# Late key weights and output weights of the first layer: split beside the projections and kept in scratch, in place of split beside the attention

## The chip, the cores and the metric

The program runs on one core of a Trainium2 chip. The metric is the device time of one execution in microseconds; before the change it is 3276.54 us, the median of three runs from 3276.2 to 3276.81 us. A profiled execution is one more run, in which a hardware profiler records the start and end of each instruction on the tensor engine (PE, with its weight loads as PEld), the vector engine (DVE), the scalar engine (ACT), GpSimd (POOL) and the queues that issue transfers; nearly all of these stand on the queue of SyncE (SP).

## The reference

A streaming encoder with two layers takes 2048 prompt rows and 64 sample rows of 1024 numbers, in 16 heads of 64. Layer A is attention over a band of 576 positions with a softmax; layer B is a strictly causal stick-breaking attention. What the change touches is the first layer's projection and its gated output:

```python
def a_project(x, g, w_in):
    h = rms_norm(x, g)
    q, k, v, gate = jnp.split(h @ w_in, 4, axis=-1)
    return split_heads(q), split_heads(k), split_heads(v), gate

def gated_out(o, gate, w_out):
    b, t = o.shape[:2]
    return (o.reshape(b, t, D_MODEL) * jax.nn.silu(gate)) @ w_out
...
            op = chunk_band_prompt(qp, kp, vp, rel_bias_a[i])
            xp = xp + gated_out(op, gp, w_out_a[i])
```

All is in 32-bit floats.

## The kernel before

**Numbers in two parts.** The matrix products run in a 32-bit matmul format of lower precision. Each operand is cut into a head, which that format holds, and a rest, the difference; a product is head by head, head by rest and rest by head. A cut is one ACT instruction (the head) and one DVE instruction (the rest): `split` (L209), or `scaled_split` (L213), which multiplies the weights by the norm's gains and goes through a 128x1024 block of weights in eight pieces of 128x128.

**Four stages.** Layer A's projections (values first, then keys, queries and gates by pairs of heads, 24 jobs), layer A's attention, layer B's projections, layer B's attention. In the trace the keys of layer A begin at 213 us, its attention runs from about 689 to 1300 us, layer B's projections to about 2020 us, and layer B's attention to the end.

**Beside the projections** (`projections`, L239) small staged tasks are handed out to the 24 jobs (`stages.pop(0)`): they cut caches and value differences and write them to scratch in device memory. In layer A they are 56: 8 caches, 8 biases, 32 value differences, 8 blocks of layer B's cached keys. In layer B they end with 16 `stage_w_out` tasks (L486), which load half of a 128-row block of layer B's output weights, cut it, and store head and rest.

**Late work beside the attention.** Products that the first items of the attention do not need are put off. `DEFER` (L42) names them: layer A's keys, layer B's gates and queries, for the second half of the prompt. `late_job` (L736) makes one such product for one pair of heads: `load`, for layer A also the four `cut` steps, then two chunks of matmuls into `ps_j`, their cut into `sp` and stores, and for some chunks a sum `lkn` (on POOL) with its turn to rows. `lkn` takes over a buffer of `sp`, so it waits until stores of `sp` have landed. After the late jobs come eight `w_out_steps` (L805) that fill the two big tiles with the output weights, then `out_steps`. The class `Beat` (L900) weaves them in: one beat is one tile of scores, and `RATE` 0.4 steps of late work fall on a beat of layer A.

**Where the weights come from** depends on `KEPT = "b"` (L43). For layer B, `projections` stores the cut weights of `DEFER` to scratch right after the cut (L381), `late_job.load` fetches head and rest, and `w_out_steps` fetches the pieces that `stage_w_out` left. For layer A, `late_job.load` fetches the weights as they are (`lraw`, 512 KB) and `cut` makes `lwh` and `lwl` beside the attention; `w_out_steps` fetches `woraw` (512 KB) for each of eight blocks and cuts it into the big tiles.

**What sets the order.** A list scheduler fixes each engine's order from a model of times; during the attention the steps of late work that stand in `in_place` keep their program order. At run time each engine, and SP's queue too, goes strictly in its order: a load that waits for its buffer, or for an earlier transfer, holds every transfer behind it.

Of the kernel before, what the change touches and what calls it, by code (L numbers as in the profile page):

```python
# [9 lines left out]
F32 = mybir.dt.float32  # L10
F32R = mybir.dt.float32r
# [5 lines left out]
P = 128  # L17
D = 1024
NK = D // P
# [13 lines left out]
CH = 512  # L33
# [6 lines left out]
SAMPLE = {(1, 0): [4, 3], (3, 2): [2, 1, 0]}  # L40

DEFER = dict(a=[("k", hp) for hp in range(HP)], b=[(k, hp) for k in "gq" for hp in range(HP)])  # L42
KEPT = "b"  # L43

RATE = dict(a=0.4, b=0.3)
LAG = dict(a=3, b=5)
# [4 lines left out]
STEP = 2  # L51
# [19 lines left out]
def f32(ap):  # L71
    return ap.bitcast(F32)
# [28 lines left out]
def encoder_step(ctx: ExitStack, tc: tile.TileContext, a: dict, o: dict):  # L101
    nc = tc.nc
# [39 lines left out]
    dram = ctx.enter_context(tc.tile_pool(name="scratch", bufs=1, space=DRAM))  # L142
# [5 lines left out]
    opool = ctx.enter_context(tc.tile_pool(name="out", bufs=1))  # L148
# [7 lines left out]
    def big_pair():  # L156
        return [big.tile([P, NK, D], F32R, name=f"big{i}", tag=f"big{i}") for i in range(2)]
# [13 lines left out]
    lay = {}  # L171
    for L, rows in (("a", CACHE_A), ("b", PAST)):
        lay[L] = dict(


            q=[dram.tile([3, P, T], F32R, name=f"q_{L}{i}") for i in range(HP)],
            k=[dram.tile([2, P, T + rows], F32R, name=f"k_{L}{i}") for i in range(HP)],

            v=dram.tile([T + rows, H, P], F32R, name=f"v_{L}"),
            g=[dram.tile([P, T], F32, name=f"gate_{L}{i}") for i in range(HP)],  # L180

            o=[dram.tile([HP, P, CH if g < GROUPS else NS], F32, name=f"o_{L}{g}") for g in range(GROUPS + 1)],

            w={x: dram.tile([2, P, NK, P], F32R, name=f"w_{L}{x[0]}{x[1]}") for x in DEFER[L] if L in KEPT},
        )

    vraw = dram.tile([1 + T, D], F32, name="v_raw")
    x1d = dram.tile([T, D], F32, name="x1")

    wod = [dram.tile([P, 2, D], F32R, name=f"wo_{k}") for k in range(NK)]  # L190
# [18 lines left out]
    def split(hi, lo, src):  # L209
        act.activation(hi, src, AF.Copy)  # L210
        dve.tensor_tensor(lo, src, f32(hi), ALU.subtract)

    def scaled_split(hi, lo, src, g):  # L213
        for k in range(src.shape[1]):
            act.activation(hi[:, k], src[:, k], AF.Copy, scale=g[:, k : k + 1])
            dve.scalar_tensor_tensor(lo[:, k], src[:, k], g[:, k : k + 1], f32(hi[:, k]), ALU.mult, ALU.subtract)
# [278 lines left out]
    def stage_bias(hp, pool):  # L495
# [231 lines left out]
    def job_steps(L, jobs, x2, first, prompt):  # L727

        return [
            late_job(L, *job, hp, x2, first, prompt)  # L730
            for hp in range(HP)
            for job in jobs
            if (job[0], hp) in DEFER[L]
        ]

    def late_job(L, kind, w, c0, g, hp, x2, first, prompt):  # L736
# [60 lines left out]
        behind = []  # L797
# [4 lines left out]
        cuts = [] if L in KEPT else [partial(cut, k0) for k0 in range(0, NK, STEP)]  # L802
        return [in_place(x) for x in [load] + cuts], products, behind

    def w_out_steps(src, w):  # L805

        raws = {}
# [10 lines left out]
        def load(k):  # L818
            if k < NK:
                tag = ("oh", "ol")[k % 2]  # L820
                raws[k] = opool.tile([P, D], F32, name="woraw", tag=tag, bufs=2)
                sp.dma_start(raws[k], src[k * P : (k + 1) * P])
# [9 lines left out]
        return [  # L832
            (
                [in_place(partial(load, i)) for i in range(3)] if k == 0 else [],
                [None],
                [[in_place(partial(cut, k)), in_place(partial(load, k + 3))]],
            )
            for k in range(NK)
        ]

    def out_steps(L, g, w, residual, done):

# [225 lines left out]
    staged_b += [partial(stage_w_out, k, half) for k in range(NK) for half in range(2)]  # L1068
# [18 lines left out]
    with (  # L1087
# [11 lines left out]
        beat.beside += w_out_steps(a["w_out_a"][0], w_out)  # L1099
        order.on = False  # L1100

        def done_a(t, n, xr, c):
# [160 lines left out]
    with (  # L1263
# [46 lines left out]
        beat.beside += w_out_steps(None, w_out)  # L1310
# [235 lines left out]
```

## Time and profile before

| | |
|---|---|
| median of 3 runs | 3276.54 us |
| profiled execution, span | 3278.2 us |
| PE busy | 3204.2 us, 98% |
| DVE busy | 1887.0 us, 58% |
| ACT busy | 1711.4 us, 52% |
| POOL busy | 1291.4 us, 39% |
| moved by transfers | 688.41 MB, mean 210 GB/s |
| mean granted PE clock | 0.994 |

The profiled execution is 1.7 us longer than the median of the runs. A share of busy time is a mean over four stages; in the projections PE is busy without a gap, in the attention ACT and DVE work beside it at about four fifths of the time. The end of a matmul is modelled and matmuls overlap, so a busy PE says only that it had work; its idle time and its clock say what was lost. In the view of windows each row gives busy microseconds and instructions of each engine, the granted clock, the busy share of the 16 DMA engines and their rate.

### The profile page before, as it was taken

How to read it: one execution, taken by the hardware profiler on the slowest of the kernel's cores; microseconds unless marked ns; L12 is line 12 of the kernel's file. 1: busy time of each engine (PE TensorE's matmuls, PEld its weight loads, DVE VectorE, ACT ScalarE, POOL GpSimd, SP SyncE). 2: the span in 40 equal slices, each digit the busy share in tenths (PEclk: the TensorE clock that was granted, in tenths of full speed). 3: DMA queues.
4: the chain of work that ended last, by engine and by line, in shares of the span. 5: the costliest groups of instructions: out<-in, count | busy, mean ns of one | idle time of the engine just before them, and what ended most of it. 6: DMA issues, size and time to landing. Idle time of an engine off the chain costs nothing.

```text
span 3278.2 us, 53687 instructions
## 1 busy us (share of the span) xinstructions
PE 3204.2 (98%) x17928; PEld 2791.0 (85%) x17928; DVE 1887.0 (58%) x3786; ACT 1711.4 (52%) x3719; POOL 1291.4 (39%) x1950
## 2 busy tenths in 40 slices
PE   8999999999998999999999999999999989999999
PEld 7889999988887898878889998788888878888877
DVE  4235431147778775231044333788878878888873
ACT  5234222258888776143134442566666656666662
POOL 3001110026665554020044200444477766877761
PEclk9999999999999999999999999999999999999999
DMA  6359993387899983553399999977735566455423
GB/s 202 121 185 368 349 331 118 117 237 220 240 260 267 252 237 130 164 174 128 113 357 352 348 357 328 251 217 217 213 121 148 162 203 174 124 143 141 138 72 119
DMA packets 464892, 688.41 MB, mean 210 GB/s; under 512 B 51446, under 2 KB 261398, under 8 KB 464615
## 3 DMA queue, kind: packets, MB, share of 16 engines
q1 hardware_dynamic: 405158, 633.85, 61.8%
q10 hardware_dynamic: 59456, 51.13, 4.8%
q8 instruction: 143, 2.34, 0.3%
q14 instruction: 135, 1.10, 0.1%
HBM read 408.78 MB, written 276.07 MB: 209 GB/s over the span
## 4 chain that ended last, share of the span: by engine, by line
PE 75%; issue 7%; DVE 6%; DMA 6%; ACT 2%; POOL 2%; SPq 1%; POOLq 0%; ACTq 0%; DVEq 0%
PE ps_t L90 23%; PE ps_v L90 11%; PE acc L90 10%; PE z L90 9%; PE wt L90 8%; PE ps_j L90 6%; PE ps_o L90 5%; DVE s L90 3%; DVE pl L90 2%; DMA vt<-v_b 1%; PE ps_tr L90 1%; ACT ph L90 1%; DMA kt<-k_b 1%; POOL s L90 1%; ACT s L90 1%
## 5 line engine op out<-in xcount | busy, mean ns | idle before, releaser
L90 DVE TENSOR_TENSOR pl<-wt,ph 128x512 fp32r<-128x512 f32 (+1 forms) x864 | 551.9, 654 | 122.4 <-ACT ph L90 118.7
L90 ACT ACTIVATE ph<-wt 128x512 fp32r<-128x512 f32 (+1 forms) x864 | 485.7, 578 | 205.4 <-PE wt L90 178.2
L90 PE MATMUL ps_t<-x_own,wh 128*128 128x362 f32 (+1 forms) x2304 | 567.5, 327 | 0.0
L90 PE MATMUL wt<-ident,s 128*128 128x128 f32 x3472 | 551.5, 274 | 13.4 <-DVE pl L90 6.8
L90 PEld LDWEIGHTS wt<-ident,s 128*128 128x128 f32 x3472 | 418.6, 141 | 88.3 <-DVE pl L90 12.9
L90 ACT ACTIVATE f<-z 128x512 f32<-128x512 f32 (+4 forms) x680 | 355.1, 535 | 196.1 <-PE z L90 139.7
L90 PEld LDWEIGHTS ps_t<-x_own,wh 128*128 128x128 f32 x2304 | 405.0, 188 | 1.8
L90 POOL TENSOR_TENSOR s<-f,s 128x256 f32<-128x256 f32 x416 | 361.3, 870 | 104.2 <-DVE s L90 95.9
L90 PE MATMUL acc<-ph,vt 128*128 128x512 f32 (+3 forms) x1088 | 376.2, 381 | 14.1 <-DMA vt<-v_b 7.5
L90 PE MATMUL z<-kt,q 128*128 128x512 f32 (+3 forms) x1280 | 375.4, 381 | 12.9 <-DMA q<-q_b 5.8
L90 PE MATMUL ps_t<-x_own,wl 128*128 128x362 f32 (+1 forms) x1152 | 376.7, 327 | 0.0
L90 PE MATMUL acc<-pl,vt 128*128 128x512 f32 (+3 forms) x1088 | 364.6, 368 | 7.2 <-DVE pl L90 6.8
L90 POOL TENSOR_SCALAR s<-s,rc 128x640 f32<-128x640 f32 (+5 forms) x264 | 199.2, 760 | 387.3 <-DMA keys<-k_a 193.3
L90 PE MATMUL ps_o<-big,oh 128*128 128x512 f32 x1088 | 336.2, 392 | 0.2 <-ACT oh L90 0.2
L90 POOL TENSOR_TENSOR two<-f 128x256 f32<-128x256 f32 x416 | 259.5, 626 | 166.3 <-ACT f L90 150.0
L90 DVE TENSOR_TENSOR_SCAN s<-two,s,own 128x256 f32<-128x256 f32 x408 | 299.7, 738 | 33.6 <-POOL two L90 32.3
L90 PEld LDWEIGHTS z<-kt,q 128*128 128x128 f32 x1280 | 221.9, 192 | 43.5 <-ACT f L90 11.8
L90 PE MATMUL ps_j<-big,lwh 128*128 128x512 f32 x768 | 246.9, 397 | 1.1 <-DVE pl L90 0.6
L90 PE MATMUL ps_t<-big,wh 128*128 128x512 f32 x768 | 238.9, 391 | 0.0
L90 PEld LDWEIGHTS ps_o<-big,oh 128*128 128x128 f32 x1088 | 202.2, 188 | 41.3 <-ACT oh L90 0.4
L90 PEld LDWEIGHTS acc<-ph,vt 128*128 128x128 f32 x1088 | 198.7, 192 | 37.1 <-ACT ot L90 8.4
L90 DVE CUSTOM_DVE_ANT_0 s<-z,bias 128x640 f32<-128x640 f32 (+4 forms) x256 | 184.7, 733 | 77.2 <-PE wt L90 51.1
(148 smaller groups left out, 5528.9 us busy)
## 6 DMA issues: line engine op xcount, KB each, us to landing
vt<-v_b SPq DMA_DIRECT2D x80, 512.0 KB, 4.9
v_b<-vs SPq DMA_DIRECT2D x64, 512.0 KB, 5.7
q<-q_a SPq DMA_DIRECT2D x128, 256.0 KB, 5.9
q<-q_b SPq DMA_DIRECT2D x128, 256.0 KB, 4.6
vt<-v_a SPq DMA_DIRECT2D x48, 512.0 KB, 7.1
kt<-k_b SPq DMA_DIRECT2D x96, 256.0 KB, 5.6
keys<-k_a SPq DMA_DIRECT2D x80, 256.0 KB, 7.1
v_a<-vs ACTq DMA_DIRECT2D x32, 512.0 KB, 2.7
```

What stands on the lines that cost most here:

```text
L90: ins = op(*args, **kwargs)
```

## The change

The distinction by `KEPT` goes: both layers keep cut weights in scratch. Beside layer A's projections the weights of the eight late keys are stored after their cut (16 stores of 512 KB), and 16 tasks `stage_w_out` for layer A's output weights are added to the staged ones, which are now 72 on 24 jobs. Beside layer A's attention a late job loads head and rest (two loads of 512 KB in place of one) and has no `cut`; a step of `w_out_steps` is two loads of 512 KB into the big tiles, in place of one load of 512 KB and two cuts of 128x512.

```diff
-KEPT = "b"
...
-            w={x: dram.tile([2, P, NK, P], F32R, name=f"w_{L}{x[0]}{x[1]}") for x in DEFER[L] if L in KEPT},
+            w={x: dram.tile([2, P, NK, P], F32R, name=f"w_{L}{x[0]}{x[1]}") for x in DEFER[L]},
...
-    def stage_w_out(k, half, pool):
+    def stage_w_out(L, k, half, pool):
         raw = pool.tile([P, CH], F32, name="vcur", tag="vr", bufs=2)
         cols = slice(half * CH, half * CH + CH)
-        nc.sync.dma_start(raw, a["w_out_b"][0][k * P : (k + 1) * P, cols])
+        nc.sync.dma_start(raw, a[f"w_out_{L}"][0][k * P : (k + 1) * P, cols])
         vs = pool.tile([P, 2, CH], F32R, name="vs", tag="vs", bufs=2)
         split(vs[:, 0], vs[:, 1], raw)
-        nc.sync.dma_start(f32(wod[k][:, :, cols]), f32(vs))
+        nc.sync.dma_start(f32(wod[L][k][:, :, cols]), f32(vs))
...
         def load():
-            if L not in KEPT:
-                st["raw"] = opool.tile([P, NK, P], F32, name="lraw", tag="og", bufs=1)
-                c = c0 + hp * P
-                sp.dma_start(st["raw"], w[:, c : c + P].rearrange("(k p) c -> p k c", p=P))
             st["wh"] = opool.tile([P, NK, P], F32R, name="lwh", tag="oh", bufs=2)
             st["wl"] = opool.tile([P, NK, P], F32R, name="lwl", tag="ol", bufs=2)
-            if L in KEPT:
-                for i, part in enumerate((st["wh"], st["wl"])):
-                    sp.dma_start(f32(part), f32(lay[L]["w"][kind, hp][i]))
-
-        def cut(k0):
-            ks = slice(k0, k0 + STEP)
-            scaled_split(st["wh"][:, ks], st["wl"][:, ks], st["raw"][:, ks], g[:, ks])
+            for i, part in enumerate((st["wh"], st["wl"])):
+                sp.dma_start(f32(part), f32(lay[L]["w"][kind, hp][i]))
...
-        return [in_place(x) for x in [load] + cuts], products, behind
+        return [in_place(load)], products, behind
...
         def parts(k):
             if k == 0:
                 w.extend(big_pair())
             for i in range(2):
-                sp.dma_start(f32(w[i][:, k]), f32(wod[k][:, i]))
-
-        if src is None:
-            return [([], [None], [[in_place(partial(parts, k))]]) for k in range(NK)]
+                sp.dma_start(f32(w[i][:, k]), f32(wod[L][k][:, i]))
...
-        def cut(k):
-            if k == 0:
-                w.extend(big_pair())
-            for c in range(0, D, CH):
-                cols = slice(c, c + CH)
-                split(w[0][:, k, cols], w[1][:, k, cols], raws[k][:, cols])
-            del raws[k]
...
+    staged += [partial(stage_w_out, "a", k, half) for k in range(NK) for half in range(2)]
```

The scheduler makes a new order from it. Three places matter below. In the rows, a line number one smaller is only the line that went with `KEPT`.

The first is POOL at the start of layer A's attention (`s` is a tile of softmax weights, `lkn` the sum of the first late job). Before:

```order
L90 TENSOR_TENSOR vprev<-vprev,vcur 128x512 x26
L90 TENSOR_SCALAR s<-s,rc 128x640 x2
L90 TENSOR_TENSOR lkn<-sp 128x512
L90 TENSOR_SCALAR s<-s,rc 128x640 x6
L90 TENSOR_SCALAR s<-s,rc 128x128
```

And with the change:

```order
L89 TENSOR_TENSOR vprev<-vprev,vcur 128x512 x26
L89 TENSOR_SCALAR s<-s,rc 128x640 x4
L89 TENSOR_TENSOR lkn<-sp 128x512
L89 TENSOR_SCALAR s<-s,rc 128x640 x4
L89 TENSOR_SCALAR s<-s,rc 128x128
```

`lkn` stands behind four tiles `s` instead of two.

The second is SP's queue at the same start, up to the stores `k_a<-sp` for which `lkn` waits. Before:

```order
L134 DMA keys<-k_a_90 64x2x512 x4
L134 DMA bias<-bias_168 128x1280
L134 DMA vt<-v_a 128x4x256
L408 DMA gate_a_105<-sg 128x1024
L134 DMA vt<-v_a 128x4x256
L134 DMA gt<-gate_a_98 128x512
L127 DMA k_a_89<-sp 128x512 x4
L134 DMA q<-q_a_81 64x2x512 x2
L90 DMA lraw<-in_w_in_a 128x8x128
```

And with the change:

```order
L133 DMA keys<-k_a_90 64x2x512 x2
L89 DMA lwh<-w_ak_112 128x1024
L89 DMA lwl<-w_ak_112 128x1024
L407 DMA gate_a_105<-sg 128x1024
L133 DMA keys<-k_a_90 64x2x512 x2
L133 DMA bias<-bias_184 128x1280
L133 DMA vt<-v_a 128x4x256 x2
L133 DMA gt<-gate_a_98 128x512
L126 DMA k_a_89<-sp 128x512 x2
L89 DMA lwh<-w_ak_113 128x1024
L89 DMA lwl<-w_ak_113 128x1024
L126 DMA k_a_89<-sp 128x512 x2
```

Two loads of the second late job now stand ahead of the stores, and two of the third between them; the second job's single load stood ahead of the first `q` before.

The third is SP's queue in the middle of layer A's attention, where the output weights come in (`o_a<-ot` stores a finished piece of attention output). Before:

```order
L90 DMA woraw<-in_w_out_a 128x1024
L134 DMA q<-q_a_83 64x2x512 x2
L134 DMA vt<-v_a 128x4x256
L90 DMA woraw<-in_w_out_a 128x1024
L134 DMA vt<-v_a 128x4x256
L90 DMA woraw<-in_w_out_a 128x1024
L134 DMA vt<-v_a 128x4x256
L127 DMA o_a_108<-ot 128x512
```

And with the change:

```order
L89 DMA big_10496<-wo_a_172 128x1024
L89 DMA big_10497<-wo_a_172 128x1024
L133 DMA keys<-k_a_91 64x2x512
L133 DMA q<-q_a_83 64x2x512 x2
L133 DMA vt<-v_a 128x4x256
L89 DMA big_10496<-wo_a_170 128x1024
L89 DMA big_10497<-wo_a_170 128x1024
L89 DMA big_10496<-wo_a_171 128x1024
L89 DMA big_10497<-wo_a_171 128x1024
L133 DMA vt<-v_a 128x4x256 x2
L126 DMA out_a_k_p<-lkn 128x4x128
L126 DMA o_a_108<-ot 128x512
```

In this piece three loads of weights have become six, and all six stand ahead of the store `o_a_108`. Between the start of these loads and this store stand twelve of the sixteen loads, where seven of the eight stood before; two more follow ahead of the first load `og` of the output stage.

More of the change, by code (lines that the diff above doesn't have):

```diff
@@ L188, in encoder_step @@
     x1d = dram.tile([T, D], F32, name="x1")
-    wod = [dram.tile([P, 2, D], F32R, name=f"wo_{k}") for k in range(NK)]
+    wod = {L: [dram.tile([P, 2, D], F32R, name=f"wo_{L}{k}") for k in range(NK)] for L in "ab"}
     biasd = [dram.tile([P, 2, 640], F32, name=f"bias_{i}") for i in range(HP)]
@@ L729, in job_steps @@
         return [
-            late_job(L, *job, hp, x2, first, prompt)
+            late_job(L, job[0], hp, x2, first, prompt)
             for hp in range(HP)
@@ L734, in job_steps, with late_job @@
         ]
[L736 removed]
+    def late_job(L, kind, hp, x2, first, prompt):
         st = {}
         def load():
[L740 to L743 removed]
             st["wh"] = opool.tile([P, NK, P], F32R, name="lwh", tag="oh", bufs=2)
             st["wl"] = opool.tile([P, NK, P], F32R, name="lwl", tag="ol", bufs=2)
[L746 to L752 removed]
+            for i, part in enumerate((st["wh"], st["wl"])):
+                sp.dma_start(f32(part), f32(lay[L]["w"][kind, hp][i]))
         def some(c, k0):
@@ L801, in late_job, with w_out_steps @@
         products = [partial(some, c, k0) for c in chunks for k0 in range(0, NK, STEP)]
-        cuts = [] if L in KEPT else [partial(cut, k0) for k0 in range(0, NK, STEP)]
-        return [in_place(x) for x in [load] + cuts], products, behind
-    def w_out_steps(src, w):
-        raws = {}
+        return [in_place(load)], products, behind
+    def w_out_steps(L, w):
         def parts(k):
@@ L812, in parts @@
             for i in range(2):
-                sp.dma_start(f32(w[i][:, k]), f32(wod[k][:, i]))
-        if src is None:
-            return [([], [None], [[in_place(partial(parts, k))]]) for k in range(NK)]
[L818 to L822, printed above, removed]
-        def cut(k):
-            if k == 0:
-                w.extend(big_pair())
-            for c in range(0, D, CH):
-                cols = slice(c, c + CH)
-                split(w[0][:, k, cols], w[1][:, k, cols], raws[k][:, cols])
-            del raws[k]
[L832 to L839, printed above, removed]
+                sp.dma_start(f32(w[i][:, k]), f32(wod[L][k][:, i]))
+        return [([], [None], [[in_place(partial(parts, k))]]) for k in range(NK)]
     def out_steps(L, g, w, residual, done):
@@ L1067, in encoder_step @@
         staged_b += [partial(stage_diff, "new", t, half), *keys_b[8 + i : 9 + i]]
-    staged_b += [partial(stage_w_out, k, half) for k in range(NK) for half in range(2)]
+    staged_b += [partial(stage_w_out, "b", k, half) for k in range(NK) for half in range(2)]
     jobs_a = [("k", w_a, D, gs["a"]), ("q", w_a, 0, gs["a"]), ("g", w_a, 3 * D, gs["a"])]
@@ L1098, in encoder_step @@
         beat.beside = job_steps("a", jobs_a, x2, NP - CACHE_A, o["a_k_p"])
-        beat.beside += w_out_steps(a["w_out_a"][0], w_out)
+        beat.beside += w_out_steps("a", w_out)
         order.on = False
@@ L1309, in encoder_step @@
         beat.beside.insert(1, end_values())
-        beat.beside += w_out_steps(None, w_out)
+        beat.beside += w_out_steps("b", w_out)
         order.on = False
```

## The prediction

> **What bounds the kernel now.** The page's first part and the view of windows were read first: who is busy, and where PE is not.
>
> ```profile
> PE 3204.2 (98%) x17928; PEld 2791.0 (85%) x17928; DVE 1887.0 (58%) x3786; ACT 1711.4 (52%) x3719; POOL 1291.4 (39%) x1950
> 250.00:300.00 50.00, 50.00 (x312) 49.93 (x311) 26.96 (x75) 21.38 (x61) 6.58 (x8) 1.00 1.06 377
> 500.00:550.00 50.00, 50.00 (x272) 46.21 (x271) 6.30 (x18) 11.89 (x30) 0.00 (x0) 1.00 0.29 104
> 700.00:750.00 50.00, 45.01 (x270) 39.81 (x271) 34.24 (x104) 35.93 (x89) 27.59 (x34) 0.93 0.72 211
> 750.00:950.00 200.00, 193.96 (x1218) 171.60 (x1216) 152.57 (x442) 164.47 (x399) 120.36 (x141) 1.00 0.84 236
> 950.00:1050.00 100.00, 91.29 (x598) 82.12 (x596) 83.40 (x208) 85.78 (x186) 57.21 (x63) 0.98 1.00 277
> 1050.00:1250.00 200.00, 198.09 (x1308) 180.58 (x1306) 150.55 (x391) 153.67 (x338) 106.67 (x122) 1.00 0.86 238
> ```
>
> PE is the bound. In layer A's projections (two rows) it never stops, whatever ACT, DVE and the transfers do beside it. Layer A's attention loses a little, unevenly. Once all late weights are in (1050 to 1250 us) PE idles 1.91 us in 200, which I take as the floor, 0.48 us in 50. Against that floor three stretches lose more:
>
> - 700 to 750 us: 4.99 us idle and 0.07 x 50 = 3.5 us of clock, less 0.5: **8.0 us**.
> - 750 to 950 us, the late keys: 6.04 idle less 1.9: **4.1 us**.
> - 950 to 1050 us, the output weights: 8.71 idle and 0.02 x 100 = 2 of clock, less 1.0: **9.7 us**.
>
> So all that the change can win in the attention is about 22 us, 0.7% of the time. Next, what ends these waits: the waits of PE from 690 to 970 us (first row) and from 975 to 1045 us (the other three), and rows of the timelines.
>
> ```profile
> PE wt L90 <- POOL s L90: 4.7, 1, 4.7
> PE acc L90 <- ACT ot L90: 5.0, 3, 2.8
> PE z L90 <- DVE mn L90: 1.7, 2, 1.5
> PE wt L90 <- DVE pl L90: 1.3, 2, 0.9
> ```
> ```profile
> 702.41 1.26 POOL L90 TENSOR_TENSOR lkn<-sp 128x512 f32<-128x512 f32 x1 [7.65 <-DMA k_a<-sp]
> 1019.51 0.53 PE L90 MATMUL acc<-ph,vt 128*128 128x512 f32 x1 [2.79 <-ACT ot L90]
> ```
> ```profile
> 1000.57 9.24 DMA woraw<-in_w_out_a
> 1009.88 8.91 DMA o_a<-ot
> 1018.87 0.60 ACT ot L90
> ```
>
> At 700 us one wait of 4.7 us: POOL stood 7.65 us at `lkn` until a store had landed, and the tiles `s` for which PE waited stood behind it. At 1019 us, in the chain of waits, a transfer too: a load of output weights lands, SP can then issue the store of `ot`, that takes 8.91 us, ACT gets its buffer back, and PE has waited 2.79 us. Only the last two waits, 3.0 us, are for ACT's and DVE's own work.
>
> **The change part by part.**
>
> *What goes from the attention.*
>
> ```profile
> L90 DVE SCALAR_TENSOR_TENSOR lwl<-lraw,g_a,lwh 128x128 fp32r<-128x128 f32 x64 | 30.3, 510 | 28.7 <-ACT lwh L90 28.2
> L90 ACT ACTIVATE lwh<-lraw,g_a 128x128 fp32r<-128x128 f32 x64 | 21.7, 392 | 9.2 <-PE ps_t L90 9.2
> L90 DVE TENSOR_TENSOR big<-woraw,big 128x512 fp32r<-128x512 f32 x16 | 11.7, 755 | 0.3 <-ACT big L90 0.3
> L90 ACT ACTIVATE big<-woraw 128x512 fp32r<-128x512 f32 x16 | 9.3, 628 | 0.0
> ```
>
> ACT loses 31 us of work and DVE 42 us, none of it PE's. Most of the keys' cuts fall between 700 and 950 us, where ACT is at 82% and DVE at 76%; without them both come below what 1050 to 1250 us shows (77% and 75%), the floor. Late keys are therefore worth up to the whole 4.1 us; some of the excess is the jobs' other work (`sp`, `lkn`), which stays. Bounds -4 and, since their loads now block SP until the job before last has ended, +1. I take **-3**.
>
> *What the loads cost.* The price of a packet comes from two queue rows, one of 520 to 600 us (nearly all 512-byte packets of `wraw`) and one of 100 to 190 us (packets of 3.6 KB on average):
>
> ```profile
> q10 hardware_dynamic: 4160, 2.10, 9.5%
> q10 hardware_dynamic: 2290, 8.33, 23.5%
> ```
>
> 0.095 x 16 x 80 us / 4160 = 29 ns, and 0.235 x 16 x 90 us / 2290 = 148 ns; by the line through both, 165 ns for 4 KB. So `lraw` (1024 packets of 512 bytes) takes 1.9 us of all 16 engines, a load of 4 KB packets (128) 1.3 us. A late job goes from 1.9 to 2.6 us, 0.7 us more in some 37: nothing at a busy share of 0.84. The output weights go from 8 x 1.3 to 16 x 1.3, 10.6 us more, where the share is already 1.00.
>
> *The start, 700 to 750 us.* With `lkn` behind four tiles, tiles three and four no longer wait for a store, and the transposes that stood for 4.7 us can run. The stores of `sp` come later, though: two loads (2.6 us) now stand ahead of them, and one was issued earlier before, so `lkn` ends near 706 instead of 703.7 us, and tile five is what can be late next. Also the second job's first matmuls now need loads issued near 684 us that land 9 to 10 us later, about when PE arrives. Gone completely: -8. Gap kept and 2.6 us longer: +3. I take half of the gain, **-4**.
>
> *The output weights, 950 to 1050 us.* The 3.0 us of waits for ACT and DVE should go. Up to the store `o_a_108` five more loads are in the queue, 6.6 us. From 960 to 1012 us SP waited for compute only so much, which is all that can absorb it:
>
> ```profile
> SPq L90 <- PE ps_j L90: 5.0, 1, 5.0
> SPq L134 <- PE z L90: 1.8, 2, 1.4
> SPq L134 <- PE wt L90: 1.8, 4, 0.7
> SPq L134 <- PE acc L90: 1.4, 3, 0.7
> ```
>
> The first is ahead of the loads and stays; the other 5.0 us may cover some of 6.6. A store that lands 2 to 6 us later lengthens the 2.79 us gap by as much, and the clock then falls. What such a gap costs is in the rows after two gaps of layer A, and in two of layer B, where the same kind of loads (two of 512 KB a step) is seen, the 50 us around a gap and the 10 after it:
>
> ```profile
> 700.00:710.00 10.00, 5.50 (x22) 4.96 (x23) 3.59 (x13) 3.68 (x10) 5.15 (x7) 0.66 0.83 242
> 1020.00:1030.00 10.00, 10.00 (x60) 8.93 (x59) 9.07 (x22) 9.68 (x21) 6.45 (x8) 0.84 0.72 177
> 2650.00:2700.00 50.00, 43.47 (x247) 36.19 (x245) 37.58 (x62) 30.23 (x60) 34.68 (x66) 0.90 0.88 259
> 2690.00:2700.00 10.00, 6.76 (x28) 5.97 (x29) 4.02 (x6) 3.86 (x7) 4.58 (x11) 0.54 1.07 314
> ```
> ```profile
> PE acc L90 <- DMA vt<-v_b: 7.5, 2, 5.3
> ```
>
> After 4.7 us of waiting 0.34 x 10 = 3.4 us were lost, after 2.79 us 1.6 us, after 5.3 us in layer B 4.6 us. So: -3 for the cuts, +4 for later landings, +2 of clock, **+3**. Bounds: -9.7, if ACT and DVE were behind all of it, to +11, what layer B's burst cost (6.5 idle and 5 of clock in 2650 to 2700 us).
>
> [...]
>
> *The projections.* Sixteen stores of kept keys, 21 us of all DMA engines, come into 213 to 320 us, where the share is 1.06. They need only land before the buffers of `wh` are written again, two jobs or some 20 us later. Layer B does the same beside its own projections, at a full DMA share, and PE has no gap:
>
> ```profile
> 1850.00:1900.00 50.00, 50.00 (x312) 49.92 (x310) 17.66 (x44) 21.88 (x60) 2.62 (x2) 1.00 0.99 337
> 200.00:250.00 50.00, 48.82 (x281) 46.02 (x280) 22.22 (x67) 22.44 (x61) 2.17 (x5) 1.00 0.78 256
> ```
>
> But staged caches are turned on PE, in order, and one late load already costs 1.18 us (second row). The 16 tasks `stage_w_out` cost some 10 us of ACT and 11 of DVE (16 x 628 and 16 x 690 ns, the forms above) and some 33 us of DMA, in a stretch where ACT is at 24%, DVE at 13% and the DMA share 0.29; if that cover were gone, the keys' first loads would start late. Bounds 0 and +10; I take **+1**.
>
> *Sum:* -4 - 3 + 3 + 1 = -3 us on the profiled execution's 3278.2, so 3275.2; its median lies 1.7 lower: **3273.5 us**.
>
> **The rivals.** *The burst is covered.* In the middle of 950 to 1050 us ACT and DVE are nearly full:
>
> ```profile
> 1000.00:1010.00 10.00, 8.63 (x63) 7.33 (x61) 9.54 (x24) 9.64 (x23) 7.46 (x7) 1.00 1.05 275
> ```
>
> If the losses there were mostly theirs, the term turns to -4, the start to -7, the keys to -4 and the projections to +1: -14, 3262.5 us. For it: cuts of 628 and 755 ns stand between PE and its operands there. Against it: the chain at 982 to 1019 us is transfers.
>
> *Slower: the burst of output weights.* The mechanism is layer B's: loads hold SP's queue, a load of `vt` or a store of `ot` lands late, PE stops and its clock falls. The place is 1000 to 1030 us; the price +11; it decides from the point where the store lands some 5 us later than now. With the start at +1, keys -3, projections +1: +10, 3286.5 us. For it: DMA share 1.00 already. Against: only five of the extra loads precede the store, and SP has 5 us of slack.
>
> *Staging jams the projections.* Key stores push caches back, PE waits for several of eight turns: +10 in place of +1, so +6, 3282.5 us. Layer B's row speaks against it.
>
> **How the numbers follow.** Forecast 0.40 (own range 3268 to 3280), covered 0.30, burst 0.19, jam 0.11. No difference below 0.2%, 6.5 us, can be told from none here: faster is below 3270, slower above 3283. Faster: 0.2 of the forecast and nearly all of the covered case, 0.36. Slower: 0.05 of the forecast, 0.8 of the burst, 0.45 of the jam, 0.22. Same: 0.42. The range takes in both larger cases but for their far ends: 3261 to 3287.
>
> **What would show it.** Right: no wait of PE for `s` near 700 us and a clock above 0.9 there; under 3 us idle in 750 to 950 us; at 1000 to 1030 us a longer wait for `ot` or a wait for `vt`, with none left for `mn` and `pl`; 50.00 busy through the projections. Wrong: `lkn` still ahead of a needed tile; matmuls `ps_j` waiting for `lwl`; a clock at 1.00 at 1020 us; gaps of PE before `ps_c` near 230 to 320 us. A change of the time in layer B's stages would be none of these steps.

## The result, and the profile after

The change makes the kernel slower: 3301.59 us, median of five runs (3298.96 to 3306.81), against 3276.81 us beside it. The ratio is 1.007, with a 95% interval of 1.006 to 1.0081. The forecast was 3273.5 us in a range of 3261 to 3287.

The profiled execution of the change has a span of 3304.7 us, 26.5 more than before's 3278.2; it is the longest of its five runs, and the medians differ by 24.8. Where the 26.5 us lie is read from four points of PE's own work that both kernels have: its start, the first scores of layer A on `keys`, the last turn of a late job's `lkn`, the last scores of layer A on `keys`, and the end.

| stretch, us | before | change | difference | predicted |
|---|---|---|---|---|
| layer A's projections, to the first scores | 688.8 | 697.6 | +8.8 | +1 |
| to the last turn of `lkn` (start, late keys) | 318.3 | 310.2 | -8.1 | -7 |
| to the last scores on `keys` (output weights) | 266.7 | 290.8 | +24.1 | +3 |
| the rest, layer B above all | 2004.4 | 2006.1 | +1.7 | 0 |

Two stretches lose 32.9 us, and one gains 8.1. First who is busy (part 1 of the page), and then windows of the change; the windows are moved with the start of the attention, so that the second to fourth rows answer to before's 688.8 to 748.8, 748.8 to 948.8 and 998.8 to 1098.8 us. The columns are as before: length, busy us of PE, PEld, DVE, ACT and POOL with their counts, granted clock, share of the transfer engines, GB/s.

```profile
PE 3208.6 (97%) x17928; PEld 2797.1 (85%) x17928; DVE 1855.6 (56%) x3722; ACT 1691.5 (51%) x3655; POOL 1285.4 (39%) x1950
```
```profile
300.00:350.00 50.00, 43.38 (x234) 40.09 (x233) 23.29 (x58) 16.43 (x43) 10.55 (x11) 0.93 1.01 358
...
697.60:757.60 60.00, 55.13 (x321) 47.41 (x320) 36.02 (x109) 38.96 (x92) 28.53 (x35) 0.97 0.87 272
757.60:957.60 200.00, 197.25 (x1245) 175.74 (x1244) 137.72 (x413) 155.76 (x367) 119.47 (x142) 1.00 0.86 243
...
1007.60:1107.60 100.00, 73.70 (x453) 66.94 (x452) 55.70 (x142) 56.62 (x122) 37.61 (x43) 0.86 0.92 254
```

And before, the start of the attention and the stretch with the output weights:

```profile
688.80:748.80 60.00, 54.76 (x318) 47.84 (x317) 39.71 (x118) 41.82 (x100) 28.59 (x35) 0.94 0.78 230
998.80:1098.80 100.00, 93.39 (x609) 83.85 (x609) 79.55 (x199) 79.90 (x176) 52.81 (x58) 0.98 0.93 263
```

PE's work is what it was. DVE lost 31 us of work and ACT 20, off PE's path. Late keys: 2.75 us idle in 200 where 6.04 stood. Around the output weights: 26.3 us idle in 100 where 6.6 stood, 19.7 more. The clock of 0.86 is a mean over the whole window, idle time included, so it cost PE less than 14 us; of the stretch's 24.1 us some 4 are left for it. In the projections, where PE before had no gap after 250 us (438.80 us busy of the 438.80 to the first scores), 6.6 us idle in 50.

What PE waited for, in the view of waits: 300 to 350 us, 700 to 750, and 990 to 1110.

```profile
PE ps_c L89 <- DMA kr<-in_cache_a_k: 5.0, 1, 5.0
...
PE ps_j L89 <- DMA lwh<-w_ak: 2.9, 1, 2.9
PE ps_j L89 <- DMA lwl<-w_ak: 1.1, 1, 1.1
...
PE z L89 <- DVE pl L89: 10.3, 1, 10.3
PE acc L89 <- ACT ot L89: 9.4, 2, 8.5
PE ps_o L89 <- ACT oh L89: 6.5, 1, 6.5
```

At 700 us the wait for `s` is gone and loads have taken its place. The 10.3 us are put down to DVE, but DVE stood too. Rows of the timelines, the landing time of the store, and SP's longest wait from 990 to 1012 us:

```profile
992.65 1.32 POOL L89 TENSOR_TENSOR ot<-ot,gt 128x512 f32<-128x512 f32 x1
1007.89 0.33 SPq L126 DMA_DIRECT2D o_a<-ot  x1
1019.94 0.22 DVE L89 TENSOR_TENSOR ot<-total,otmp 64x64 f32<-64x64 f32 x1 [9.13 <-issue]
1022.26 1.41 PE L89 MATMUL z<-keys,q 128*128 128x320 f32 x4 [10.26 <-DVE pl L89]
```
```profile
DMA to landing us min/median/max: 12.0/12.0/12.0
```
```profile
SPq L133 <- DMA big<-wo_a: 5.3, 3, 2.3
```

POOL finished a piece `ot` at 993.97 us. SP issued its store at 1007.89, 14 us later, behind other transfers that waited for earlier ones to land: from 990 to 1012 us SP stood 5.3 us until output weights had landed (the row above), and 6.4 us until keys, `kt` and values had. The store landed 12.0 us after its issue, at 1019.9, when DVE got the buffer for the next `ot`; the cut `pl` and the next minima stood behind DVE's instruction, and PE behind them. The next store of `ot` (1032.42 us, 7.82 us) made the 8.5, and a late `og` the 6.5.

### The profile page after: what moved, and what is told of

Its sections match the earlier page's. It is cut to its first block, busy times and chain, and to the rows that moved or that the text cites. A ratio compares the mean times of both kernels' runs of the same rounds, so it can differ in the third digit from the quotient of the medians.

```text
span 3304.7 us, 53687 instructions
## 1 busy us (share of the span) xinstructions
PE 3208.6 (97%) x17928; PEld 2797.1 (85%) x17928; DVE 1855.6 (56%) x3722; ACT 1691.5 (51%) x3655; POOL 1285.4 (39%) x1950
## 4 chain that ended last, share of the span: by engine, by line
PE 70%; issue 8%; DVE 5%; DMA 5%; ACT 2%; POOL 1%; SPq 0%; ACTq 0%; POOLq 0%; DVEq 0%
PE ps_t L89 21%; PE acc L89 11%; PE z L89 10%; PE wt L89 9%; PE ps_j L89 7%; PE ps_v L89 6%; PE ps_o L89 5%; DVE s L89 2%; DVE pl L89 2%; DMA vt<-v_b 1%; ACT ph L89 1%; DMA q<-q_a 1%; DMA q<-q_b 0%; PE ps_n L89 0%; PE ps_c L89 0%
```

## The experiments

Fifteen kernels were run, each with a profile and four to eleven runs, in turn with the kernel before on the same chip. Their edits are shown shortened. The table gives medians, the median of before on the same chip, the ratio with its interval, the three first stretches of the profiled execution as above, and PE's idle time in the 100 us around the loads of output weights (998 to 1098 us, or up to 12 later where the attention starts later). The stretches of the profiled executions vary by 2 to 3 us where nothing was changed (687.6 to 690.3 for the first). The scheduler makes a new order for each kernel, so an edit can also move what it does not name. In e6, e9, e12 and e13 output products have moved from the third stretch to behind it, so it can't be set beside the others there.

| kernel | us | before | ratio | 1st | 2nd | 3rd | idle |
|---|---|---|---|---|---|---|---|
| the change | 3301.6 | 3276.8 | 1.0070 [1.0060, 1.0081] | 697.6 | 310.2 | 290.8 | 26.3 |
| e1 keys only | 3290.7 | 3278.8 | 1.0033 [1.0020, 1.0045] | 701.0 | 314.0 | 269.3 | |
| e2 output weights only | 3295.4 | 3278.8 | 1.0048 [1.0035, 1.0060] | 687.0 | 316.7 | 286.8 | 21.2 |
| e3 half the bytes | 3281.1 | 3278.8 | 1.0002 [0.9993, 1.0011] | 689.9 | 309.1 | 272.6 | 11.7 |
| e4 on ACT's queue | 3307.4 | 3278.8 | 1.0087 [1.0073, 1.0100] | 700.9 | 325.3 | 278.2 | |
| e5 keys only, two tasks | 3279.6 | 3279.3 | 1.0002 [0.9994, 1.0011] | 688.7 | 312.4 | 269.9 | 9.1 |
| e6 single loads, two tasks | 3288.3 | 3279.3 | 1.0027 [1.0016, 1.0038] | 688.1 | 308.6 | - | 16.1 |
| e7 before, two tasks | 3280.6 | 3279.3 | 1.0006 [0.9997, 1.0015] | 690.3 | 319.1 | 265.0 | |
| e8 third buffer for ot | 3302.1 | 3279.3 | 1.0071 [1.0057, 1.0084] | 700.2 | 310.8 | 286.6 | 22.9 |
| e9 single loads, spread more | 3293.2 | 3280.9 | 1.0045 [1.0031, 1.0059] | 688.8 | 312.1 | - | 17.5 |
| e10 before, with idle copies | 3293.5 | 3280.9 | 1.0039 [1.0026, 1.0051] | 688.9 | 320.4 | 279.2 | 15.3 |
| e11 as e5, third ot | 3278.9 | 3280.9 | 0.9995 [0.9987, 1.0004] | 688.9 | 313.0 | 265.7 | 4.9 |
| e12 loads late, two tasks | 3302.7 | 3278.9 | 1.0066 [1.0053, 1.0080] | 688.5 | 311.5 | - | 3.2 |
| e13 pairs apart, two tasks | 3290.7 | 3280.3 | 1.0037 [1.0025, 1.0050] | 688.8 | 312.4 | - | 17.2 |
| e14 before, one load | 3276.1 | 3280.3 | 0.9989 [0.9980, 0.9998] | 687.6 | 319.5 | 262.9 | 4.6 |
| e15 second buffer for kr | 3300.7 | 3278.6 | 1.0070 [1.0057, 1.0084] | 693.7 | 310.2 | 287.3 | 22.7 |

**Each half alone (e1, e2).**

```diff
# e1: the kernel before with
-KEPT = "b"
+KEPT = "ab"
# e2: the kernel before, with the sixteen tasks stage_w_out "a" in staged, and
-w_out_steps(a["w_out_a"][0], w_out)
+w_out_steps(None, w_out, "a")
```

> Only the late keys are kept; the output weights come in and are cut beside the attention as before. The stretches are those of the profiled execution, bounded by PE's own landmarks: up to the first scores of layer A's attention (before 688.8 us, with the whole change 697.6), from there to the last turn of a late job's sum lkn (318.3 and 310.2), from there to the last scores of layer A on keys (266.7 and 290.8), and the rest (2004.4 and 2006.1). Theory: the stores of kept keys alone delay the projections and the output weights alone the third stretch, so 697, 310, 267 and a time of 3277 to 3280 us. Rival: the staged output weights, which share the projections' queue, delay them; then 689, 310, 267 and 3268 to 3270 us.

> Only the output weights are kept; the late keys are loaded raw and cut beside the attention as before. Theory: first stretch 689 us (the staged tasks come after 500 us, where the transfers are idle), second 318, third about 291, time 3299 to 3303 us. Rival: the third stretch's loss is a collision that needs both halves of the change (the late keys' loads end later or the attention runs ahead); then it is 270 to 280 and the time 3280 to 3290 us.

In e1 the place is that of the theory, the first stretch, but each stretch is 2 to 4 us longer than it says (701.0, 314.0 and 269.3), and the time lies 11 us above its range. In e2 the stretches are near the theory's (687.0, 316.7 and 286.8), and the time, 3295.4 us, lies 4 us below its range. The two halves lose in different places, and their losses, 11.9 and 16.6 us, come to 28.5 beside the whole's 24.8. Staged output weights beside the projections cost nothing, as PE's row in e2 (687.0 us to the first scores) shows. The prices of the transfers can be read here too: part 3 of the pages, queue 1, of before, e1 and e2.

```profile
q1 hardware_dynamic: 405158, 633.85, 61.8%
```
```profile
q1 hardware_dynamic: 401446, 646.43, 62.4%
```
```profile
q1 hardware_dynamic: 412966, 650.63, 62.7%
```

Times their spans that is 2025.9, 2051.4 and 2065.7 us of all transfer engines: 25.5 us for the keys and 39.8 for the output weights. The prediction had 26.6 and 43.6. Such a difference is good to some 10 us only: e7, with the packets and bytes of before, has 61.6% of 3276.8 us, 2018.5, so 7 less. Within that the price of a transfer was right; what it does to PE was not.

**Bytes or places in the queue (e3, e4).**

```diff
# e3, for layer A: half of each store and load
-nc.sync.dma_start(f32(lay[L]["w"][kind, hp][i]), f32(part))
+nc.sync.dma_start(f32(lay[L]["w"][kind, hp][i][:, :4]), f32(part)[:, :4])
-sp.dma_start(f32(w[i][:, k]), f32(wod[L][k][:, i]))
+sp.dma_start(f32(w[i][:, k, :512]), f32(wod[L][k][:, i, :512]))
# e4, for layer A
-nc.sync.dma_start(f32(lay[L]["w"][kind, hp][i]), f32(part))
+nc.scalar.dma_start(f32(lay[L]["w"][kind, hp][i]), f32(part))
-sp.dma_start(f32(w[i][:, k]), f32(wod[L][k][:, i]))
+act.dma_start(f32(w[i][:, k]), f32(wod[L][k][:, i]))
```

> The whole change with the same number of transfers in the same places, but each store and load of a layer A late key weight moves four of its eight blocks and each load of an output weight half of its columns; the products use the halves that are there, twice, so part of the weights is left out of the computation. Theory (time of the transfer engines): the 10.6 us that the output weights add go to about zero and the keys' stores to half, so the third stretch returns to about 268 us, the first to 690 to 693, and the time is 3268 to 3274 us. Rival (places in SyncE's queue, of which each transfer takes one whatever its size): first 697, third 285 to 291, 3295 to 3302 us.

> The whole change, but ScalarE's queue issues the stores of kept keys and the loads of the output weights; the bytes are the same, and SyncE's queue has 32 transfers less. Rival (SyncE's queue): with these out of its way, 689 in the first stretch and about 268 in the third, 3268 to 3272 us. Theory (time of the transfer engines): the same bytes cross the same stretches, so about 697 and 285 to 291, 3295 to 3302 us. Below both, if ACT itself is held while its queue waits: a third stretch above 295 us with ACT as the engine waited for.

With the same number of transfers and half their bytes the time is that of before (1.0002), but above the theory's 3268 to 3274 us: the gain of the second stretch (-9.2) came, and the third stretch, 272.6 us, is 18.2 less than in the change and still 5.9 more than before (2.7 more than in e5 below, which keeps the keys alone). Of the change's waits there, the one for `ot` stayed (950 to 1120 us of e3):

```profile
PE acc L89 <- ACT ot L89: 8.9, 2, 8.0
```

So as far as e3 goes, bytes make most of the loss beside the attention. For the projections e3 says nothing: its order has some 70 matmuls between the last two turns of caches, where the change has none (see e15). In e4, with the same bytes off SyncE's queue, as much is lost as with the change, or more, 3307.4 us, above its theory's range. The attention lost 18 us as well (325.3 + 278.2 against 318.3 + 266.7); the loss only moved ahead of the last `lkn`, with waits of ACT of up to 5.6 us that are put down to transfers. Since ACT itself was held, where it now issues the loads, e4 can't tell bytes from places in a queue; that rests on e3. Whether a second queue brings engines of its own to carry the bytes, no run shows.

**The projections (e5, e7, e15).** Up to here the stores' bytes looked like the cause there too.

```diff
# e5: e1 with, and e7: before with
-for _ in range(-(-len(stages) // (len(jobs) * HP - j * HP - hp))):
+even = -(-len(stages) // (len(jobs) * HP - j * HP - hp))
+for _ in range(2 if L == "a" and j == 0 else even):
```

> Only the late keys kept, as in e1, and in addition the eight key jobs of layer A's projections hand out two staged tasks each in place of three (eight value differences move behind them, where the transfer engines have room). Theory: the kept keys' stores delayed the projections because their 21 us of all transfer engines came on top of a stretch that was already full; the eight tasks moved out carry about as much, so the first stretch is 688 to 690 us (701.0 in e1), the second and third as in e1 (314 and 269), and the time 3276 to 3280 us against 3290.7. Rival: the stores hold the caches' loads in the queue's order, whatever else is there; first stretch 697 or more, 3286 to 3291 us.

> The kernel before with the two staged tasks of e5 and nothing else: the control for e5. Theory: its only gap in the key jobs, 1.2 us before the turn of a cache, goes; otherwise nothing: 687 to 689, 318, 267, 3275 to 3279 us, no difference from before. Rival: the full transfer engines of that stretch cost the kernel before more than the gap shows; below 3272 us.

e5 removes the loss, 688.7 us, and e7 shows that this is no gain of its own (690.3; its one wait before the turn of a cache, which was expected to go, stayed, 1.7 us). The transfer engines are a little less full in e5 than in e1, 0.98 and 347 GB/s against 1.00 and 360, and as full as before (0.98, 346). This alone doesn't settle whether bytes were the cause. Windows from 225 to 480 us, of e1 and of e5:

```profile
225.00:480.00 255.00, 244.21 (x1367) 229.78 (x1366) 104.46 (x285) 84.01 (x228) 36.12 (x33) 0.98 1.00 360
```
```profile
225.00:480.00 255.00, 254.44 (x1437) 240.56 (x1436) 108.31 (x291) 85.34 (x235) 30.19 (x29) 1.00 0.98 347
```

PE's fixed order showed what else differs. In the change and in e1 the turns of two caches stand directly behind each other; before and in e5 78 to 104 rows of matmuls lie between the last ones. In e4 some 8 do, and PE waited 8.5 us. The change's order at the last two caches of layer A, near 334 us, and before's at the first of these two:

```order
L89 MATMUL ps_t<-big_200,wl 128x512
L89 MATMUL ps_c<-ident,kr 128x128 x8
L89 MATMUL ps_n<-ident,kf 64x128 x4
```
```order
L90 MATMUL ps_t<-x_own_182,wh 128x364
L90 MATMUL ps_c<-ident,kr 128x128 x4
L90 MATMUL ps_t<-x_own_183,wh 128x364
```

A cache block is turned from `kr`, which has one buffer. Its next load can't be issued before the turn is done, so with nothing between the turns PE waits for a whole load. The timelines of the change show just that:

```profile
334.71 0.60 PE L89 MATMUL ps_c<-ident,kr 128*128 128x128 f32 x4
335.34 0.38 SPq L433 DMA_DIRECT2D kr<-in_cache_a_k  x1
340.30 1.09 PE L89 MATMUL ps_c<-ident,kr 128*128 128x128 f32 x4 [4.99 <-DMA kr<-in_cache_a_k]
```

In e1 the same load was issued at 337.07 us and PE waited 8.62 us. The last run gave `kr` a second buffer and left the rest of the change:

```diff
-kr = pool.tile([P, 4, P], F32, name="kr", tag="kr", bufs=1)
+kr = pool.tile([P, 4, P], F32, name="kr", tag="kr", bufs=2)
```

> The whole change, with a second buffer for kr, the raw cache block that PE turns; stores, tasks and bytes as in the change. Theory (the wait is the one buffer: in the change's order two turns of caches are back to back on PE, so the second load can start only when the first turn is done, and its 5 us pass with PE idle): first stretch 687 to 690 us in place of 697.6, attention as in the change, 3290 to 3296 us. Rival (the bytes of the kept keys' stores): 695 to 700, 3298 to 3305 us.

The wait for `kr` is gone, and the first stretch is 693.7 us, between the two theories: about half of the loss is left. It is a new wait, in the view of waits from 200 to 480 us of e15, and behind its 3.4 us stands a late store of cached values (third row, a timeline):

```profile
PE ps_n L89 <- DVE kl L89: 3.4, 1, 3.4
PE ps_n L89 <- POOL kf L89: 1.4, 1, 1.4
267.32 0.84 ACT L89 ACTIVATE sh<-ps_t 128x364 fp32r<-128x364 f32 x2 [11.17 <-DMA v_a<-vs]
```

The median, 3300.7 us, is above the theory's range and can't be told from the change's; the profiled execution of e15 is the fastest of its five runs (3295.2 us), that of the change the slowest, so the 3.9 us between their first stretches are no measure of a gain. So the named wait is shown to be the one buffer. What the rest is, in this other order, and what part the key stores have in it, was not settled.

**The output weights: when and how close (e6, e9, e12, e13).** All four keep both kinds of weights and hand out two tasks as e5 does, so e5's 3279.6 us is what they are to be compared with. They ran on other chips than e5, e6 excepted, so each difference is good to some 5 us.

```diff
# the steps of w_out_steps("a"); parts(k, i) is one load, both(k) two
-[([], [None], [[both(k)]]) for k in range(NK)]
# e6
+[([], [None], [[parts(k, i)]]) for k in range(NK) for i in range(2)]
# e9
+[([], [None], [x]) for load in loads for x in ([load], [])]
# e12
+[([], [None], [[]]) for _ in range(32)] + [([], [None], [[both(k)]]) for k in range(NK)]
# e13
+[([], [None], [x]) for pair in pairs for x in ([pair], [])]
```

> The whole change, with the two staged tasks of e5 in the key jobs, and each output weight load is a step of its own (16 steps of one load in place of 8 of two), so the same bytes come over about twice the time. Theory A (the loads cost because they come together in a stretch that is full): first stretch 689, third 268 to 278, 3278 to 3288 us. Theory B (more bytes cost as much wherever they come beside this attention, since PE waits for transfers all along): first 689, third 285 to 291, 3290 to 3296 us.

> As e6, but an empty step follows each of the 16 loads of output weights, so the same bytes come over about four times the time of the change (32 steps in place of 8). PE lost 26.3 us of idle time in the 100 us around the loads with the change, 16.1 in e6, 6.6 before. Theory A of e6 (the loads cost because they come together): under 10 us in any such 100 us, and 3276 to 3282 us. Theory B (each load costs wherever it comes, e6 only moved part of it): the idle time of the whole attention stays as in e6, and 3286 to 3290 us.

> Both kinds of weights kept and the two staged tasks of e5; the output weights come in the change's eight steps of two loads, but 32 empty steps stand ahead, so they begin near 1170 us, in the last 100 us of layer A's attention, where the transfer engines of the kernel before are at 0.8 and then at 0.22. The output products that stood between the scores move behind the attention, where PE had no gap in e9. Theory A (loads cost only where the transfers are full, 980 to 1160 us): that stretch loses no more than in e5 (9 us in 100), and the time is that of e5 or somewhat less, 3276 to 3282 us. Theory B (each load beside the attention costs its 1.3 us or more): 3286 to 3293 us.

> As e6, but the loads of output weights stay in pairs and an empty step follows each pair: the same bytes over the same 16 steps. Theory P (a pair holds up everything behind it for twice as long, and what is loaded ahead covers one load but not two): more than 20 us idle in the 100 us around the loads, 3294 to 3302 us. Theory Q (only the transfer time in the stretch counts): as e6, 14 to 18 us idle there and 3285 to 3291 us.

The sixteen loads are issued over 82 us in the change (977.1 to 1059.3 us), 109 in e6, 102 in e13, 191 in e9 and 67 in e12. Over e5 they cost 8.7 us (e6), 11.0 (e13), 13.6 (e9) and 23.1 (e12). Theory P fell: pairs are no worse than singles within the noise. Of the theories A and B neither holds whole, and the times of e9 and e12 lie above the ranges of both. Somewhat further apart halves the loss; still further apart doesn't lower it (e9); and closer together in a later place costs as much as in the change. Three windows of e12, and the second of them before:

```profile
998.00:1098.00 100.00, 96.77 (x697) 90.54 (x695) 86.58 (x232) 92.65 (x207) 65.39 (x76) 1.00 1.01 269
1098.00:1198.00 100.00, 81.02 (x545) 74.74 (x543) 70.04 (x191) 73.94 (x166) 52.16 (x63) 0.90 1.01 275
1198.00:1298.00 100.00, 90.77 (x510) 79.80 (x511) 49.85 (x113) 49.73 (x104) 30.80 (x33) 0.92 0.49 154
```
```profile
1098.00:1198.00 100.00, 98.55 (x648) 89.53 (x647) 74.41 (x192) 76.11 (x167) 51.51 (x60) 1.00 0.87 232
```

The stretch in which the change lost its 26 us loses 3.2 us here, with the transfer engines at 1.01 but without the loads. It is not the place, and a share of 1.01 alone does not stop PE. The loss followed the loads to 1098 us and beyond, where the share before had been 0.87. They were issued at 1123.9 to 1191.0 us, earlier than the expected 1170; so no run tried what they cost where the transfer engines are nearly idle.

**Which wait (e8), which bytes (e10, e14).**

```diff
# e8: the change, and e11: e5, with
-sums["ot"] = pool.tile([P, CH], F32, name="ot", tag="ot", bufs=2)
+sums["ot"] = pool.tile([P, CH], F32, name="ot", tag="ot", bufs=3 if L == "a" else 2)
# e10: before, with a copy behind each load; nothing reads spare
 sp.dma_start(raws[k], src[k * P : (k + 1) * P])
+sp.dma_start(spare[k], src[k * P : (k + 1) * P])
# e14: before, with one load
-if k < NK:
+if 0 < k < NK:
+    raws[k] = raws[0]
+elif k == 0:
```

> The whole change with a third buffer for ot, the piece of finished attention output, so ACT and DVE need not wait until the store before last has landed. Theory A (the late store of ot is the link through which the loads stop PE): first stretch 697 to 701 as in the change, third 270 to 280 in place of 290.8, 3281 to 3292 us. Theory B (the stretch lacks transfer time, and without this wait PE stops at the next late load, of q, vt or og): third 284 to 291, 3295 to 3302 us.

> The kernel before, which cuts the output weights beside the attention, and after each of its eight loads of them SyncE issues a copy of the same 512 KB within device memory that nothing waits for. So the transfers grow by about what the change adds there, and nothing else of the change is in it. Theory (transfer time alone stops PE): third stretch 280 to 287 us against 266.7, 3290 to 3297 us. Rival (the loss needs what the change does to the order: its loads in pairs ahead of the stores of ot, or that the weights come into the tiles that the products use): third stretch under 271 us, 3277 to 3282 us.

> The kernel before, but only the first of the eight blocks of layer A's output weights is loaded; all eight cuts are made from it, so the other seven blocks are left out of the computation. It takes 9.3 us of transfers out of the stretch. Theory linear (each load costs its transfer time and more, as the eight added ones did): 3264 to 3270 us, and less than 3 us lost in 950 to 1050 us. Theory threshold (there is room for eight loads, and the wait of 1019 us in the kernel before is the first sign of its end): 3274 to 3279 us, a few us gone at most.

In e8 the wait for `ot` is gone and PE stands at the next late transfers instead, from 950 to 1120 us:

```profile
PE z L89 <- DMA q<-q_a: 12.7, 2, 6.9
PE ps_o L89 <- ACT oh L89: 9.7, 1, 9.7
```

So the store of `ot` is only where the lateness came out. In e10 nothing of the change is left but added transfers that nothing waits for (the scheduler moved some 40 of ACT's 3714 instructions as well), and the third stretch is 279.2 us, 12.5 more, the time 12.6 more: the stretch lies just under the theory's range and the time inside it, both far from its rival's. In e14, whose engines keep the order of before, seven loads fewer save 4.3 us, and 3276.1 us is in the threshold theory's range. One load, eight and sixteen thus stand at -4, 0 and +9 to +24 us. Before could not have saved much more, since its third stretch has only 8.0 us of idle time and some 2 of clock to lose; the added loads cost more than that.

**A version that was to beat both (e11).**

> e5 (late keys kept, two staged tasks in the key jobs) with a third buffer for ot: a version that could beat both. In e5 PE still waits 7.3 us for ot between 950 and 1120 us. Theory: without the 10.6 us of added loads there is transfer time left, so the wait goes and not much takes its place; third stretch 262 to 266 us against 269.9, 3272 to 3276 us. Rival: as in e8 the wait moves to the loads of q or og, third 268 to 271, 3278 to 3281 us.

The third stretch is 265.7 us and the wait for `ot` 1.3 us in place of 7.3; here the buffer helps, in the order of e5. The time, 3278.9 us, is not the theory's 3272 to 3276, and the ratio, 0.9995 with an interval of 0.9987 to 1.0004, can't be told from no change. No kernel of the study is shown to be faster than before but e14, which leaves work out.

## Why the prediction was wrong, step by step

- *The start, 700 to 750 us (-4): right in mechanism, smaller in size.* The wait for `s` is gone. The loads of the second job were late where the text had them "land 9 to 10 us later, about when PE arrives": 4.0 us of waits for `lwh` and `lwl`, one of its signs of being wrong. In 60 us PE was idle 4.9 us in place of 5.2, and the clock was 0.97 in place of 0.94: 1 to 2 us gained.
- *Late keys (-3): right.* 6.04 us idle became 2.75, -3.3; "under 3 us idle" held. The whole stretch gained 8.1 beside the predicted 7 partly by luck: some 3 us of it came after these windows, ahead of the last `lkn` (3.3 us idle before, 0.6 with the change), where the text had such a gain too, but counted it to the output weights.
- *The output weights (+3, from -9.7 to +11): the step that failed.* The loss was +24.1 us in the whole, +20.1 in e2 alone. The text priced the loads right, 10.6 us of transfers, and then followed them to one store, counted five loads ahead of it, and set 5 us of SP's slack against 6.6. The runs showed no such single link. Three waits of 6.5 to 10.3 us came, in e8 others in their place, and e10 lost 12.6 us by transfers that nothing waits for. The text charged the added loads to one store; they delay the other transfers of the stretch too.
- *The upper bound, +11 from layer B.* It was taken from another stage's loss at a share of 0.88; it bounded nothing here.
- *The projections (+1, from 0 to +10): failed in size, inside its bounds.* It was +8.8 (+12.2 in e1, outside them). The cover named for it, layer B without a gap at a full share, was no cover: it told of bytes, and the longest wait, 5.0 us, came from the order, two turns of caches through one buffer. That order could be read ahead; the prediction quoted the orders of POOL and SP and not that of PE beside the projections.
- *The rivals.* The slower rival had the right mechanism and place, at less than half the price. The jam had about the right price for its stage, +10, with one turn waiting 5.0 us where it had several. They were set up as alternatives with 0.19 and 0.11, but they lie in different stages and both came. Even their sum, 11 and 10 less the 8.1 gained, is 13 us, about half of the 24.8 measured; the other half is the burst's price.
- *The clock (+2).* In the change the 4.99 us gap at 335 us is followed by this row:

```profile
340.00:350.00 10.00, 9.10 (x41) 8.32 (x42) 5.99 (x12) 2.96 (x7) 3.05 (x4) 0.69 0.99 337
```

0.31 of 9.10 busy us are 2.8 us. The prediction's 1.6 to 4.6 us are too high at the upper end: it took the clock's loss of all 10 us, and so counted idle time twice. Of busy time alone its three rows give 1.9 us (0.34 of 5.50), 1.6 and 3.1 (0.46 of 6.76), and the 3.5 us of clock at 700 to 750 us become 3.2. The length of a gap alone did not decide: in the change one of 2.00 us at 2077.94 us is followed by half the clock (0.50 from 2080.25 to 2083.66 us), one of 2.25 us at 2726.90 us is not (1.00 from 2729.15 to 2732.57). Before, the 2.79 us gap lies in the first of these two stretches of 3.41 us, and the second has half the clock:

```profile
1016.43:1019.84 3.41, 0.62 (x4) 0.33 (x3) 0.85 (x4) 0.97 (x2) 0.73 (x2) 1.00 0.99 312
1019.84:1023.25 3.41, 3.41 (x13) 3.00 (x12) 2.53 (x6) 3.41 (x9) 2.63 (x4) 0.50 0.68 177
```

In the clock records of before and of the change 3.41 us is the shortest time at half the clock, and the others are 6.83 and 10.24 us (but for the last, which runs into the program's end). Cut into stretches of 3.41 us from where the records begin, they show PE busy for 0 to 0.43 of the time before, and 0 to 0.51 in the change, in each stretch at full clock that one at half the clock follows; in those that one at full clock follows it was busy for at least 0.50 before and 0.45 in the change.

What stays open is the rate of exchange: 10.6 us of added transfers cost between 9 and 23 us, and neither the distance of the loads nor their place alone orders these numbers. That the buffers let transfers run ahead of PE by about one load's time, that the first eight loads use up this lead, and that PE pays for what comes after, would fit e14, e10, e8 and the 3.2 us of e12's first window; it was argued and not shown. A rival stands beside it. In the traces of before and of the change each issue of SP comes only when the transfer issued eight before it has landed (945 of the 945 with a recorded landing before, 1211 of 1211 with the change; with seven in place of eight 0.83 and 0.82 of them). So an added load also takes one of eight places, from its issue to its landing (in the median 8.7 us from 960 to 1060 us of the change), and not 1.3 us alone. No run changed the number of places. Nor was a third `ot` tried with spread loads, though in e13 16.4 us of PE's waits from 950 to 1120 us are for `ot`.

## What to carry to other kernels

Charge added transfers to the whole stretch, not to the one wait in the trace that they lengthen: price them against what the stretch can still take, and find that by taking loads out and putting copies in (e14, e10), since the busy share doesn't tell (1.01 with 3 us lost, 0.92 with 26). Rivals that lie in different stages are terms of one sum, not alternatives. When a scheduler remakes the order, read it for neighbours that share a single buffer, on the bound engine and in each stage that is touched.

## What was not expected of the hardware

The transfer engines were at a mean share of 1.01 over 100 us while PE lost 3.2 us, and at 0.92 while it lost 26.3: the share alone doesn't say whether transfers come ahead or late. The sum of all packet times is a poor measure of what was added, too. The copies of e10 (512 KB within device memory each, 4.19 MB more on queue 1) made the third stretch 12.5 us longer; yet the sum over all packets grew by only 2.5 us (61.6% of 3292.8 us against 61.8% of 3278.2), less than the 7 us by which it differs between before and e7.
